# Branch projections of a hybrid decoder layer: from sixteen plain column tiles per set to four plain tiles and six pairs by seven block products

## The chip, the cores and the metric

The kernel runs on one core of a Trainium2 chip. The metric is the device time of one execution in microseconds; before the change the median of three runs is 3235.01 us (3234.76 to 3237.45).

## The reference, cut to what matters

One decoder layer on 576 tokens (512 of a prompt, 64 of samples), all in f32:

```python
u = einsum('bld,de->ble', rmsnorm(x, norm_w), w_in)        # z, xbc, dt, q, k, v, g_attn, mix_s, mix_a
y = gated_group_rmsnorm(ssd(conv(xbc), ...) + d_skip * xs, z)   # 576 x 4096
o = attention(q, k, v) * silu(g_attn)                           # 576 x 2048
p_ssm  = einsum('bli,id->bld', y, w_ssm_branch)                 # 4096 -> 2048
p_attn = einsum('bla,ad->bld', o, w_attn_branch)                # 2048 -> 2048
merged = sigmoid(mix_s) * p_ssm + sigmoid(mix_a) * p_attn
x = x + einsum('bld,de->ble', merged, w_out)
```

A final rmsnorm gives the outputs. This case is about `p_attn`, `p_ssm` and `merged`.

## The kernel before, in words

Everything is stored transposed: a tile has 128 features in the partitions and the tokens along the free axis, in two halves of 288 tokens. A product of f32 precision is made of three fp32r matmuls: a weight block W is split into `wh` (a copy on ACT, L75) and `wl` (a subtraction on DVE, L76), the activations likewise into `ah` and `al`, and TensorE adds `wh*ah + wh*al + wl*ah`. Weights come in chunks of 1024 x 128 (512 KB, `raw`, two buffers, L68), split into `wh`/`wl` (three buffers each).

There are two ways to multiply. **Plain** (`run_main`, matmuls at L338): a column tile of 128 output features has two chunks of 8 steps, and a step has three matmuls on each half of the tokens, so a tile is 2 x 8 x 3 x 2 = 96 matmuls of 288 columns. **Pairs** (`run_pairs`, matmuls at L442): two column tiles and the two halves of both the inputs and the tokens form a 2x2 block product that is done with seven block products instead of eight (the Winograd form of Strassen's method), each of 8 x 3 matmuls of 288 columns, so a pair is 168 matmuls where two plain tiles are 192. For it DVE makes four sums of weight blocks (S1 to S4, L382), seven weight blocks are split instead of four, and the results are put together by adds on eviction (L396, L401). The activation sums are made once per set of activations.

The order of the work: `FIRST` = 6 gate tiles ("mixes": sigmoid of one column tile of mix_a or mix_s, stored in DRAM as `ma_d`/`ms_d`), during which `sums_job` makes the activation sums; then 24 pairs for g_attn and z; then K, V, dt, and the four attention groups, with 13 mixes between them (`MIXES`); then the conv and scan groups, with 8 mixes between them (`MIXES_S`) and five behind the last. Attention and scan run as generators that are advanced by `pump()` after every step (lists `jobs`, paced, and `quick`, one advance per step), so that their small work lies between the matmuls; `drain()` at the end of a stage advances what is left. The tile scheduler puts instructions in order by program order and readiness, and each engine and each DMA queue then works strictly in that order.

Then the branch projections: `split_acts` loads o (16 row tiles of 128x576, L1261) and splits them into the 16 pairs `ah`/`al` (L1269 on ACT, L1270 on DVE); 16 plain tiles of `w_attn`; for each half of y the same, with 16 plain tiles of `w_ssm`. `gate` evicts: it loads the gate (L1329), multiplies on DVE (L1331, L1333) and adds into `mrg` (L1334), which stays in SBUF. So there are three sets of 16 plain tiles. Beside the first set the residual rows (`res_job`, L1308) and the final norm's weight `fw` (L1337) are loaded. Last come `w_out` (twice 16 plain tiles, one token span each), transposes, residual add and final norm.

## Time and profile before

| what | value |
|---|---|
| median of three runs | 3235.01 us (3234.76 to 3237.45) |
| the profiled execution | 3234.26 us |
| its span, first to last instruction | 3232.5 us |
| TensorE (PE) busy | 3145.6 us, 97% |
| VectorE (DVE) busy | 1782.0 us, 55% |
| ScalarE (ACT) busy | 1386.3 us, 43% |
| GpSimd (POOL) busy | 349.6 us, 11% |
| mean granted TensorE clock, as a share of full | 0.987 |
| bytes moved by DMA | 431.59 MB, mean 134 GB/s |

The busy share is an average over stages. A view by windows tells what an engine did in one stage (busy us, and in brackets the instructions), with the granted clock, the share of time that the 16 DMA engines were busy, and GB/s. In the chain of waits one follows what ended last back to the start.

### The profile page before, as it was taken

How to read it: one execution, taken by the hardware profiler on the slowest of the kernel's cores; microseconds unless marked ns; L12 is line 12 of the kernel's file. 1: busy time of each engine (PE TensorE's matmuls, PEld its weight loads, DVE VectorE, ACT ScalarE, POOL GpSimd, SP SyncE). 2: the span in 40 equal slices, each digit the busy share in tenths (PEclk: the TensorE clock that was granted, in tenths of full speed). 3: DMA queues.
4: the chain of work that ended last, by engine and by line, in shares of the span. 5: the costliest groups of instructions: out<-in, count | busy, mean ns of one | idle time of the engine just before them, and what ended most of it. 6: DMA issues, size and time to landing. Idle time of an engine off the chain costs nothing.

```text
span 3232.5 us, 57506 instructions
## 1 busy us (share of the span) xinstructions
PE 3145.6 (97%) x23323; PEld 3035.2 (94%) x23323; DVE 1782.0 (55%) x3076; ACT 1386.3 (43%) x2603; POOL 349.6 (11%) x427
## 2 busy tenths in 40 slices
PE   7989999999999999999999999999989999999997
PEld 6989999999989989999999999999879999999997
DVE  7656666632544443367776876866842333433454
ACT  5434444432455546445556555555531221212433
POOL 3200000000000100112122122122110000000111
PEclk9999999999999999999999999999999999999999
DMA  6564444433332432445645645645673443533555
GB/s 199 145 152 121 122 124 124 116 107 89 103 101 75 122 102 86 124 113 132 182 117 156 176 125 147 173 130 147 172 245 101 125 146 106 151 104 97 163 163 157
DMA packets 699272, 431.59 MB, mean 134 GB/s; under 512 B 41016, under 2 KB 663368, under 8 KB 698816
## 3 DMA queue, kind: packets, MB, share of 16 engines
q1 hardware_dynamic: 668000, 397.50, 44.3%
q10 hardware_dynamic: 18000, 18.35, 1.9%
q0 software_dynamic: 13008, 12.09, 1.5%
q8 instruction: 183, 3.00, 0.4%
q14 instruction: 81, 0.66, 0.1%
HBM read 363.37 MB, written 74.71 MB: 136 GB/s over the span
## 4 chain that ended last, share of the span: by engine, by line
PE 87%; DMA 6%; DVE 3%; ACT 2%; issue 1%; POOL 1%; SPq 0%; ACTq 0%; DVEq 0%; POOLq 0%
PE ps L338 60%; PE ps L442 16%; PE bank L637 1%; DMA raw<-in_w_out_dram 1%; PE bank L853 1%; PE bank L594 1%; DMA raw<-in_w_in_dram 1%; PE bank L1087 1%; PE bank L1065 1%; PE bank L627 1%; PE bank L923 1%; DVE wl L76 1%; PE bank L919 1%; ACT wh L75 1%; DMA L<-nacs_d 1%
## 5 line engine op out<-in xcount | busy, mean ns | idle before, releaser
L338 PE MATMUL ps<-ah,wh 128*128 128x288 f32 (+2 forms) x5408 | 1236.7, 300 | 25.4 <-ACT craw L816 9.6
L338 PE MATMUL ps<-ah,wl 128*128 128x288 f32 (+2 forms) x5408 | 1229.6, 299 | 2.0 <-DVE wl L76 1.8
L338 PE MATMUL ps<-al,wh 128*128 128x288 f32 (+2 forms) x5408 | 1229.9, 299 | 0.3 <-DVE al L1270 0.3
L75 ACT ACTIVATE wh<-raw 128x1024 fp32r<-128x1024 f32 x538 | 569.8, 1059 | 1232.7 <-PE ps L338 801.5
L76 DVE TENSOR_TENSOR wl<-raw,wh 128x1024 fp32r<-128x1024 f32 x538 | 670.2, 1246 | 689.1 <-ACT wh L75 685.9
L338 PEld LDWEIGHTS ps<-ah,wh 128*128 128x128 f32 x5408 | 897.7, 191 | 39.3 <-issue 17.8
L338 PEld LDWEIGHTS ps<-ah,wl 128*128 128x128 f32 x5408 | 897.9, 190 | 17.5 <-issue 10.8
L338 PEld LDWEIGHTS ps<-al,wh 128*128 128x128 f32 x5408 | 897.8, 190 | 5.1 <-issue 2.4
L442 PE MATMUL ps<-ah,wh 128*128 128x288 f32 x768 | 228.1, 297 | 6.3 <-DVE w L396 6.3
L442 PE MATMUL ps<-ah,wl 128*128 128x288 f32 x768 | 228.3, 297 | 2.0 <-DVE wl L76 2.0
L442 PE MATMUL ps<-al,wh 128*128 128x288 f32 x768 | 227.9, 297 | 0.0
L442 PEld LDWEIGHTS ps<-ah,wh 128*128 128x128 f32 x768 | 145.8, 190 | 6.5 <-issue 6.5
L832 DVE SCALAR_TENSOR_TENSOR cacc<-craw,prm,cacc 128x600 f32<-128x600 f32 x144 | 127.0, 887 | 42.1 <-ACT cacc L830 40.4
L442 PEld LDWEIGHTS ps<-ah,wl 128*128 128x128 f32 x768 | 145.7, 190 | 2.5 <-DVE wl L76 2.5
L442 PEld LDWEIGHTS ps<-al,wh 128*128 128x128 f32 x768 | 145.8, 190 | 0.1
L382 DVE TENSOR_TENSOR raw<-raw 128x1024 f32<-128x1024 f32 x96 | 117.0, 1221 | 46.3 <-DMA raw<-in_w_in_dram 45.4
L870 ACT ACTIVATE L<-L,nacs_n 128x128 f32<-128x128 f32 (+1 forms) x320 | 96.6, 379 | 61.0 <-DVE L L867 60.5
L1387 POOL TENSOR_TENSOR res<-res,fw 128x128 f32<-128x128 f32 (+3 forms) x35 | 31.7, 930 | 826.3 <-ACT junk L1383 793.1
L1333 DVE TENSOR_TENSOR sg<-ps,sg 128x576 f32<-128x576 f32 x32 | 24.2, 757 | 127.0 <-PE ps L338 127.0
L598 DVE CUSTOM_DVE_ANT_0 sc<-bank,bm 128x256 f32<-128x256 f32 (+1 forms) x128 | 43.8, 388 | 80.0 <-PE bank L594 72.1
L867 DVE TENSOR_TENSOR L<-L,nacs_n 128x512 f32<-128x512 f32 (+1 forms) x80 | 54.0, 691 | 51.7 <-DMA L<-nacs_d 51.1
L911 POOL TENSOR_TENSOR xl<-xe,xh 128x512 fp32r<-128x512 f32 x32 | 56.7, 1772 | 201.1 <-ACT xh L910 182.0
(508 smaller groups left out, 3664.3 us busy)
## 6 DMA issues: line engine op xcount, KB each, us to landing
raw<-in_w_in_dram SPq DMA_DIRECT2D x306, 512.0 KB
raw<-in_w_ssm_branch_dram SPq DMA_DIRECT2D x64, 512.0 KB
raw<-in_w_out_dram SPq DMA_DIRECT2D x64, 512.0 KB
L<-nacs_d SPq DMA_DIRECT2D x64, 256.0 KB
s<-in_state_ssm_dram SPq DMA_DIRECT2D x64, 256.0 KB
out_dram<-s SPq DMA_DIRECT2D x64, 256.0 KB
raw<-in_w_attn_branch_dram SPq DMA_DIRECT2D x32, 512.0 KB
zs<-z_d SPq DMA_DIRECT2D x32, 288.0 KB
```

The source lines that it names most:

```text
L75: pin(nc.scalar.activation(wh, raw, AF.Copy))
L76: pin(nc.vector.tensor_tensor(out=wl, in0=raw, in1=wh, op=ALU.subtract))
L338: ten.matmul(sums[i][:, s, :part.shape[1]], a[:, kk, :], part, start=(k == 0 and q == 0), stop=(k == last and q == 2))
L382: vec.tensor_tensor(out=s_[x], in0=s_[a], in1=s_[b], op=op)
L442: ten.matmul(st[p]["ps", i][:, :TH], a[:, k, :], b, start=i < 4 and k == 0 and q == 0, stop=k == 7 and q == 2, skip_group_check=i >= 4)
L594: ten.matmul(ps[:, i, lo:256], qT[m, h][:, blk * P:(blk + 1) * P], ks[h // 4][d][:, blk * P - 128 + lo:blk * P + P], start=d == 0, stop=d ...
L598: vec.tensor_tensor_reduce(out=s_[:, i, lo:256], in0=ps[:, i, lo:256], in1=bm[j][:, i, lo:256], scale=1.0, scalar=-3e38, op0=ALU.add, op1= ...
L627: ten.transpose(pt[:, r * P:(r + 1) * P], sc[j][:, i, kb * P:(kb + 1) * P], ident)
L832: vec.scalar_tensor_tensor(out=acc[:, :600], in0=raw[:, i:i + 600], scalar=prm[:, i * 48 + j:i * 48 + j + 1], in1=acc[:, :600], op0=ALU.mu ...
L867: vec.tensor_tensor(out=l_[:rows, :, :n], in0=l_[:rows, :, :n], in1=nacs_n[:rows, blk, h:h + 4].unsqueeze(2).to_broadcast([rows, 4, n]), o ...
L870: act.activation(l_[:rows, i, :n], l_[:rows, i, :n], AF.Exp, scale=-1.0, bias=nacs_n[:rows, blk, h + i:h + i + 1])
L911: pool.tensor_tensor(out=xl, in0=xe, in1=xh, op=ALU.subtract)
```

## The change

The three sets are done as four plain tiles (`FIRST_OUT` = 4) and six pairs each. `run_pairs` becomes `pairs_of`, which takes the weight and its first row and returns `head` (loads, two splits and three sums of the first pair) and `run`; `run_main` takes chunks loaded earlier (`raws`) and a callback `then` that it calls ahead of the last chunk. The activations are written into the tiles `hk` of the first stage (as `hx`), the activation sums are made anew for every set by `forms_job`, merged sums go by way of `mg_d` in DRAM, and the last two mixes (`N_END`) move from the attention stage to just ahead of the first set. The residual rows and `fw` are loaded at the start of `w_out`. The first 24 pairs keep their work; there `head` is called ahead of the last chunk of the six mixes, and the split of t1 comes behind the first product.

```diff
-MIXES = (2, 2, 3, 6)
-MIXES_S = (1, 1, 1, 1, 1, 1, 1, 1)
+MIXES = (2, 2, 2, 5)
+MIXES_S = (1, 1, 1, 1, 1, 1, 1, 0)
+N_END = 2
+FIRST_OUT = 4
...
+            if then and n == len(flat) - 2:
+                then()
...
-                st[p]["ps", i] = p1.tile([P, 512], F32, tag="ps", name="ps") if i < 4 else ...
+                    st[p]["ps", i] = p1.tile([P, 512], F32, tag=f"ps{i}", name="ps") if i < 4 else ...
...
+    raws = {}
+    run_main(seq, then=lambda: raws.update({0: W.load(in_loads(ends[0][0])[0])}))
+    drain()
+    stk, tx, rs, ev = pair_pools()
+    run_main([m_in(c, by_halves(gate_out(AF.Sigmoid, d_, n))) for c, d_, n in ends], raws=raws)
...
+    def acts_in(src, ks):
+        for k in ks:
+            t_ = staged_rows()
+            sync.dma_start(out=t_[:, :T], in_=src[k * P:(k + 1) * P, :])
+            split_half(hk[k], t_[:, :T])
...
+    def forms_job(src):
+        for k in range(8):
+            u, v = staged_rows(), staged_rows()
...
+            sync.dma_start(out=u1, in_=src[k * P:(k + 1) * P, :TH])
+            sync.dma_start(out=u2, in_=src[k * P:(k + 1) * P, TH:])
+            sync.dma_start(out=v[:, :T], in_=src[1024 + k * P:1024 + (k + 1) * P, :])
+            vec.tensor_tensor(out=t1_, in0=u2, in1=u1, op=ALU.subtract)
+            act.dma_start(out=xb_d[k * P:(k + 1) * P, :], in_=t1_)
+            vec.tensor_tensor(out=t2_, in0=v2, in1=t1_, op=ALU.subtract)
+            yield
+            split_half(tt[0][k], t2_)
+            pool.tensor_tensor(out=u2, in0=v2, in1=u2, op=ALU.subtract)
+            pool.tensor_tensor(out=v1, in0=v1, in1=t2_, op=ALU.subtract)
+            yield
+            split_half(tt[1][k], u2)
+            split_half(tt[2][k], v1)
+            yield
...
+    def merge_out(gate_d, n, add, last):
+        def f(j, src, t_):
...
+            sync.dma_start(out=sg, in_=gate_d[rows, cs])
+            if add:
+                mg = etile("mg")
+                sync.dma_start(out=mg, in_=mg_d[rows, cs])
+            vec.tensor_tensor(out=t_, in0=src, in1=sg, op=ALU.mult)
+            if add:
+                pool.tensor_tensor(out=t_, in0=t_, in1=mg, op=ALU.add)
+            if last and n > 13:
+                held.append((n, cs, t_))
+            else:
+                act.dma_start(out=mg_d[rows, cs], in_=t_)
...
+    def on_products(n, t1, raws, src, w, r0, rows):
+        def f(p, i):
+            if (p, i) == (-n, 0):
+                for k in range(8):
+                    split_half(b12[k], t1[k])
+            if p < -1:
+                return
+            if i in (1, 2):
+                raws[i - 1] = W.load(w_loads(w, r0, 0)[i - 1])
+            while i > 4 and held:
+                row, cs, t_ = held.pop(0)
+                split_half([a[:, cs] for a in hk[row]], t_)
+            if i == 2:
+                acts_in(src, range(4))
+            elif i == 3:
+                acts_in(src, range(4, 8))
+            elif i == 6:
+                acts_in(src, range(8, rows))
...
+    acts_in(o_d, range(KT))
+    for i in range(3):
...
+        def last_chunk():
+            head()
+            for k in range(8):
+                t1.append(etile("x"))
+                sync.dma_start(out=t1[k], in_=xb_d[k * P:(k + 1) * P, :])
...
+        quick.append(forms_job(src))
+        run_main([(w_loads(w, r0, n * P), hx, by_halves(takes[n])) for n in range(FIRST_OUT)], raws=raws, then=last_chunk)
+        drain()
...
+        run()
...
+    quick.append(res_job(xq, (0, 1, 2)))
+    sync.dma_start(out=fw, in_=AP(final_w, 0, [[0, P], [1, D]]))
-    oa = split_acts(staged)
...
-    run_main([(w_loads(w_attn[0], 0, n * P), oa, gate(ma_d, n, False)) for n in range(KT)])
-    for hk in range(2):
-        ya = split_acts([lambda k=k: load_act(y_d, 16 * hk + k) for k in range(KT)])
-        run_main([(w_loads(w_ssm[0], D * hk, n * P), ya, gate(ms_d, n, True)) for n in range(KT)])
```

The staged rows use the pairs' pool `rs` (five buffers of 4 KB a partition), the gates, merged sums and results the pool `ev` (14 tiles of 128x288). All 32 mixes are still made.

## Rows read from the trace of the kernel before

**Rows 1.** The page: TensorE's busy share, and its busy tenths in 40 slices.

```profile
PE 3145.6 (97%) x23323; PEld 3035.2 (94%) x23323; DVE 1782.0 (55%) x3076; ACT 1386.3 (43%) x2603; POOL 349.6 (11%) x427
...
PE   7989999999999999999999999999989999999997
```

**Rows 2.** The chain that ended last: start us, us, what, how many.

```profile
198.08 475.87 PE ps L442 x3574
...
717.69 12.80 PE ps L338 x96
...
2403.95 377.99 PE ps L338 x2820
```

**Rows 3.** Windows: us, busy us (instructions) per engine, clock, DMA share, GB/s.

```profile
core 0: us, PE busy (x) PEld busy (x) DVE busy (x) ACT busy (x) POOL busy (x), PEclk, DMA share, GB/s
198.00:674.00 476.00, 475.86 (x3574) 475.63 (x3574) 322.82 (x349) 197.61 (x265) 0.00 (x0) 0.99 0.43 122
...
2360.00:2380.00 20.00, 15.30 (x96) 14.28 (x96) 8.34 (x12) 10.63 (x18) 4.08 (x4) 0.91 1.05 357
2380.00:2404.00 24.00, 15.45 (x117) 15.25 (x115) 12.96 (x17) 8.34 (x11) 0.00 (x0) 0.87 0.87 262
...
2580.00:2604.00 24.00, 24.00 (x183) 24.00 (x182) 15.68 (x19) 11.99 (x16) 0.00 (x0) 1.00 0.81 258
...
2994.00:3014.00 20.00, 20.00 (x141) 19.98 (x140) 9.85 (x16) 7.47 (x10) 0.00 (x0) 1.00 0.61 191
```

**Rows 4.** Waits of TensorE, 2340 to 2420 us: total us, times, longest.

```profile
PE ps L338 <- DVE mrg L1331: 8.5, 1, 8.5
PE bank L977 <- ACT th L970: 3.5, 1, 3.5
```

**Rows 5.** Timeline of ACT, then of POOL, about the end of attention.

```profile
1310.01 0.65 ACT L1115 ACTIVATE mix<-ps 128x576 f32<-128x576 f32 x1
...
1340.87 0.41 ACT L814 ACTIVATE craw<-ps 128x288 f32<-128x288 f32 x1 [1.40 <-DMA o_d<-oT]
...
1330.25 6.54 POOL L653 TENSOR_TENSOR oT<-oT,ga 128x576 f32<-128x576 f32 x4 [11.89 <-DVE oT L737]
```

**Rows 6.** Groups by line and shape, 200 to 660 us: busy us, mean ns.

```profile
L76 DVE TENSOR_TENSOR wl<-raw,wh 128x1024 fp32r<-128x1024 f32 x146 | 178.4, 1223 | 82.5 <-ACT wh L75 82.5
L75 ACT ACTIVATE wh<-raw 128x1024 fp32r<-128x1024 f32 x145 | 153.9, 1062 | 266.2 <-PE ps L442 259.1 <-DMA z_d<-w 6.6 <-ACT w L1125 0.5
...
L382 DVE TENSOR_TENSOR raw<-raw 128x1024 f32<-128x1024 f32 x81 | 98.9, 1221 | 22.5 <-DMA raw<-in_w_in_dram 21.7
L396 DVE TENSOR_TENSOR c<-ps,u 128x288 f32<-128x288 f32 x42 | 19.1, 454 | 21.6 <-PE ps L442 21.6
```

**Rows 7.** Timeline of DVE, then of POOL, from 2350 us: start us, us.

```profile
2350.17 2.76 DVE L962 TENSOR_TENSOR xc<-xc,zs 128x576 f32<-128x576 f32 x4
...
2356.27 1.35 DVE L76 TENSOR_TENSOR wl<-raw,wh 128x1024 fp32r<-128x1024 f32 x1 [3.35 <-ACT wh L75]
...
2351.00 2.93 POOL L964 TENSOR_TENSOR tot<-xc 128x576 f32<-128x576 f32 x1 [31.90 <-DVE xc L962]
2353.89 1.14 POOL L964 TENSOR_TENSOR sqr<-xc 128x576 f32<-128x576 f32 x1
...
2356.62 2.01 POOL L964 TENSOR_TENSOR sqr<-xc 128x576 f32<-128x576 f32 x1
2358.71 1.42 POOL L966 TENSOR_TENSOR tot<-tot,sqr 128x576 f32<-128x576 f32 x1
```

**Rows 8.** DMA issues by line: how many, KB each.

```profile
raw<-in_w_ssm_branch_dram SPq DMA_DIRECT2D x64, 512.0 KB
...
stg<-y_d SPq DMA_DIRECT2D x32, 288.0 KB
...
x<-xb_d SPq DMA_DIRECT2D x8, 144.0 KB
```

**Rows 9.** Groups by line and shape, 2410 to 2990 us.

```profile
L1270 DVE TENSOR_TENSOR al<-stg,ah 128x576 fp32r<-128x576 f32 x32 | 23.2, 756 | 9.5 <-ACT ah L1269 9.4
L1269 ACT ACTIVATE ah<-stg 128x576 fp32r<-128x576 f32 x32 | 21.5, 684 | 16.7 <-DMA stg<-y_d 15.4
```

**Rows 10.** Groups by line and shape, DVE, 66 to 130 us.

```profile
L1166 DVE TENSOR_TENSOR x<-x 128x288 f32<-128x288 f32 x24 | 10.0, 453 | 0.0
```

**Rows 11.** Windows: 140 to 190 us alone.

```profile
140.00:190.00 50.00, 45.34 (x328) 44.65 (x326) 23.85 (x25) 16.86 (x22) 12.96 (x13) 0.97 1.04 222
```

More of the change, by code (lines that the diff above doesn't have):

```diff
@@ L308, in wait, with run_main @@
             yield
-    def run_main(tiles, had=()):
+    def run_main(tiles, had=(), raws={}, then=None):
         flat = [(i, c) for i, t in enumerate(tiles) for c in range(len(t[0]))]
@@ L322, in prep @@
                 i, c = flat[n]
-                ready[n] = W.split(W.load(tiles[i][0][c]))
+                ready[n] = W.split(raws.pop(n) if n in raws else W.load(tiles[i][0][c]))
         def step(n, kk, only=(0, 1)):
@@ L355, in run_main, with pairs_of @@
             n += m
-    def run_pairs(cols, ops, takes, after=None):
+    def pairs_of(w, r0, cols, ops, takes, after):
         n = len(cols)
@@ new lines, in head, with run @@
+        def head():
+            load(0, "A11", "A21", "A22", "A12")
+            split(0, 0)
+            sum_(0, "S1")
+            sum_(0, "S2")
+            split(0, 1)
+            sum_(0, "S3")
+        def run():
+            for p in range(n):
+                for i in range(7):
+                    if i < 5:
+                        split(p, i + 2)
+                    else:
+                        split(p + 1, i - 5)
+                    if i == 1:
+                        load(p + 1, "A11", "A21", "A22")
+                    elif i == 2:
+                        sum_(p, "S4")
+                    elif i == 3:
+                        sum_(p + 1, "S1")
+                        load(p + 1, "A12")
+                    elif i == 4:
+                        sum_(p + 1, "S2")
+                    elif i == 5:
+                        sum_(p + 1, "S3")
+                    st[p]["ps", i] = p1.tile([P, 512], F32, tag=f"ps{i}", name="ps") if i < 4 else st[p]["ps", (0, 2, 3)[i - 4]]
+                    wh, wl = st[p].pop(i)
+                    for k in range(8):
+                        ah, al = ops[i][k]
+                        for q, (a, b) in enumerate(((wh, ah), (wh, al), (wl, ah))):
+                            ten.matmul(st[p]["ps", i][:, :TH], a[:, k, :], b, start=i < 4 and k == 0 and q == 0,
+                                       stop=k == 7 and q == 2, skip_group_check=i >= 4)
+                        pump()
+                    evict(p, i)
+                    after(p - n, i)
@@ L449, in hybrid @@
+        return head, run
     win = w_in[0]
@@ L1173, in hybrid @@
     mixes = [(OFF_MA + n * P, ma_d, n) for n in range(16)] + [(OFF_MS + n * P, ms_d, n) for n in range(16)]
-    quick.append(sums_job())
-    run_main([m_in(c, by_halves(gate_out(AF.Sigmoid, d_, n))) for c, d_, n in mixes[:FIRST]], first)
-    drain()
-    ops[2] = [split_half(b12[k], t1[k]) for k in range(8)]
-    ms.close()
-    ms = ExitStack()
-    p1 = ms.enter_context(tc.tile_pool(name="p1", bufs=4, space=PSUM, reuse_waits="tile"))
     cols, takes = [], []
@@ L1230, in hybrid @@
     seq.append(m_in(OFF_DT, take_dt))
-    left = [m_in(c, take_mix(d_, n)) for c, d_, n in mixes[FIRST:]]
+    left = [m_in(c, take_mix(d_, n)) for c, d_, n in mixes[FIRST:-N_END]]
+    ends = mixes[-N_END:]
     for m in range(4):
@@ L1274, in hybrid, with w_loads @@
[L1274 to L1290 removed]
+    def w_loads(w, r0, col):
+        v = w[r0:r0 + D, col:col + P].rearrange("(c k p) n -> c p k n", p=P, k=8)
+        return [v[c] for c in range(2)]
@@ new lines, in hybrid @@
+    held = []
+    def merge_out(gate_d, n, add, last):
+        def f(j, src, t_):
+            rows, cs = slice(n * P, (n + 1) * P), slice(j * TH, (j + 1) * TH)
+            sg = etile("sg")
+            sync.dma_start(out=sg, in_=gate_d[rows, cs])
[7 more added lines that the diff above has]
+                held.append((n, cs, t_))
+            else:
+                act.dma_start(out=mg_d[rows, cs], in_=t_)
+        return f
```

165 lines of the change are left out of this document (64 added, 101 removed).

## The prediction

> **What bounds the kernel now.** I read the profile's page first. TensorE is busy for 97% of the span and is at 9 in nearly every slice [rows 1], so a change pays if it takes matmuls away or fills one of the few gaps, and costs what makes TensorE wait. The chain of waits says what one matmul of 288 columns costs: 12.80 us for the 96 of a plain tile, 133.3 ns each, and 475.87 us for 3574 in the pairs, 133.1 ns, the same price [rows 2]. The windows then show the stages. In the pairs TensorE waits for nothing while DVE is at 322.82 of 476 us (68%), ACT at 42% and DMA at a share of 0.43 [rows 3]. At the start of the second set, 2580 to 2604 us, 16 row tiles are loaded and split while DMA is at 0.81, and TensorE loses nothing. At the start of the first set it does: 96 and 117 matmuls in 44 us are worth 28.4 us at 133.3 ns, so 15.6 us are lost there [rows 3]. The view of waits names 12.0 us of it: 8.5 for an eviction that waits for its gate, 3.5 for the sum of squares of the last scan group [rows 4]; the rest is mostly a clock that was granted at 0.91 and 0.87 [rows 3].
>
> **The matmuls.** A pair has 168 instead of 192. Eighteen pairs drop 432, at 133.3 ns 57.6 us; per set 16 x 12.8 = 204.8 becomes 4 x 12.8 + 6 x 22.4 = 185.6 us. TensorE is the path here, so all of it counts: **-57.6 us**.
>
> **The start of the first set.** The two moved mixes are 2 x 12.8 = 25.6 us of matmuls whose inputs are there, put exactly where 15.6 us were lost. They cover the loading and splitting of o. What stays: the 3.5 us wait, because that small product is still ahead of later matmuls in TensorE's order, and I allow 2 us because the staging buffers take over memory of the scan stage, whose last y rows are still being stored. Bounds 0 and -15.6; I take **-10.1 us**.
>
> **The end of attention** loses those two tiles. The last mix left TensorE at 1310.0, the last gate products on POOL ended at 1336.8 and the next stage's first eviction came at 1340.9, held by the store of o [rows 5]. In between TensorE had two conv tiles (25.6 us) and the small attention products. Now 32 steps fewer, times 9/8, leave 36 more advances of the attention job to the drain: about one more block of queries. Its chain is mostly small work on ACT and DVE; the same two conv tiles cover it, and it can run beside the sample part. Bounds 0 and 25.6 (no cover at all); I take **+2 us**, near the first, since the block brings matmuls of its own.
>
> **The pairs of the three sets.** DVE per pair: 7 splits at 1.223, 4 weight sums at 1.221, 5 adds and 4 gate products at 0.454 us [rows 6]: 17.5 of 22.4 us, 78% against 68% in the pairs of before. ACT has 7 x 1.062 and one copy, under 8 us; it loses four evictions. POOL gets 4 adds, each half of the 1.42 us of a 576-wide one [rows 7]: 2.8 us. SP issues four weight loads and eight small ones; per pair 4 x 512 + 12 x 144 KB [rows 8] are 3.87 MB, 173 GB/s. ACT's queue issues 4 stores, and each waits for POOL's add, with the next weight splits queued behind it. Splits run two products (6.4 us) ahead, which covers an add that waits for DVE. The gate loads have 14 buffers, a pair's worth, so they are a pair ahead. Bounds 0 and 1 us per pair; I take **+3 us** over the 12 pairs that add.
>
> **The four plain tiles of a set** are the tight place: 51.2 us in which much else falls. DMA: 10 weight chunks (three tiles, and the head of the pairs), 8 row tiles of 288 KB, 8 x 576 KB for the activation sums, 8 x 144 KB stored and loaded again, and 8 x 144 KB each of gates, merged sums and results: 17792 KB = 18.2 MB, 356 GB/s. The best window here moved 357 at a share of 1.05; the second set's start, 258 at 0.81, would be 318 if full [rows 3]. At 318 it is 57.3 us, 6.1 too many. DVE has 8 x 0.756 for the rows [rows 9], 40 x 0.453 for sums and splits [rows 10], 10 x 1.223, 3 x 1.221 and 8 x 0.454 [rows 6]: 43.6 us, 85%. ACT, with 8 x 0.684 [rows 9], 24 half-size splits under 0.684 and 10 x 1.062, stays under 33 us. Part of the bytes can slip: rows come in during the last pair, weights are two or three chunks ahead, and the sums are due one product after the other. Bounds 0 and 6.1 per set, with an excess for the slower rates among the rivals. I take 4.5 for the sets with merged sums and 3 for the first: **+12 us**. SP works in order, so a load that waits for one of the five staging buffers holds the weight chunks behind it; that is how the excess reaches TensorE.
>
> **The boundary from pairs to tiles** I cost at nothing: the first eight row tiles come free after the third product and have 12.8 us, the accumulators of the first tile are evicted early, and the first two weight chunks are loaded during the last pair. Without that cover each set would start as the first did, 15.6 us. Dropping `mrg` and its 32 adds costs and brings nothing, since DVE had room there.
>
> **The output stage** gets 2560 KB of residual rows and 1024 KB of `fw` from the first set. A step takes three matmuls, 20 us / 141 each, 0.43 us [rows 3], so six loads nine steps apart spread 3.67 MB over 23 us: 158 GB/s on top of 191. That is 349 where 191 at a share of 0.61 would be 313 if full [rows 3], so about 2.6 us late. The first transposes also wait behind these jobs, with two result buffers. Bounds 0 and 8; **+3 us**.
>
> **The first pairs.** The loads come one chunk earlier, but the 140 to 190 us stretch is at a share of 1.04 from the bias table [rows 11], and that work is unchanged. Nothing, within 3 us.
>
> **Sum** against the profiled execution: 3234.3 - 57.6 - 10.1 + 2 + 3 + 12 + 3 = 3186.6; that execution is 0.75 us below the median, so I say **3187 us**.
>
> **Rival 1: DVE and POOL stand in each other's way.** POOL's square took 2.93 us while DVE multiplied from 2350.2 to 2352.9, and 2.01 beside a split, but 1.14 when free; that split took 1.35 instead of 1.223 [rows 6, 7]. So POOL stood still while DVE worked on two operands in SBUF, and DVE a little too. If their times simply add up, the four tiles have 43.6 + 24 x 0.71 = 60.6 us in the later sets (9.4 over) and 55.0 in the first (3.8 over), 22.6 instead of 12 us; a pair has 17.5 + 4 x 1.47 = 23.4, 1.0 over, 12 instead of 3 us. That gives 3187 + 19.6 = 3207 us. For it: these rows. Against: half of it can slip to where DVE has room. The Trainium skill (SBUF — State Buffer, Who interferes with whom) speaks against this change here: a DVE instruction with two SBUF inputs and a GpSimd instruction that reads SBUF exclude each other for the whole instruction. By that rule the times add up, and the trace agrees for POOL, with 2.93 against 1.14 us.
>
> **Rival 2: the row tiles come late** at the start of each set, in the staging buffers shared with the weights. Then each set starts as the first did: 3 x 15.6 = 46.8 instead of 12 + 5.5, so 3216 us. Against it: the loss-free second start [rows 3].
>
> **Rival 3: the drain of attention lies bare,** 25.6 instead of 2 us: 3211 us. For it: the eviction held by the store [rows 5].
>
> **Rival 4, slower: DMA at its poor rate.** In the stretch of the bias table DMA was full at 222 GB/s, and TensorE lost matmuls [rows 11]. At that rate the 18.2 MB of the four tiles take 82 us, 30.8 too many, 92 us in three sets: 3187 - 12 + 92 = 3267 us. It decides from 255 GB/s down: the gain without this term is 59.7, 19.9 per set, so break-even is at 71.1 us. For it: stores to DRAM and loads of short rows mix here too. Against it: 258 GB/s at a share of only 0.81 with the same row tiles [rows 3]. That the fewer matmuls are made and the time stays is the same case at its edge.
>
> **How the numbers follow.** Forecast 0.65 (3162 to 3200), rival 1 0.17, rival 2 0.08, rival 3 0.05, rival 4 0.05. All but rival 4 are faster; a little of rivals 2 and 4 ends near 3235. A measurement of this kernel tells about 0.2% (6.5 us) from no change: faster 0.91, same 0.04, slower 0.05. The range goes from 3162 (57.6 and 15.6 gained, nothing given back) to 3214, which takes in rivals 1 and 3 and leaves out most of rivals 2 and 4.
>
> **What would show it.** Right: 432 fewer matmuls of 288 columns; no waits over a microsecond inside the pairs; DVE near 78% there; the wait for `th` of some 3.5 us and no 8.5 us one at the first set; small waits of TensorE for weight splits or `ah`/`al` in the four tiles, with DMA near full. Wrong: pairs longer than 23 us with DVE full (rival 1), waits for `ah` at each set's first steps (rival 2), for `craw` about 1310 (rival 3), or four tiles of over 70 us with DMA full below 255 GB/s (rival 4).

## The result and the profile after

The changed kernel takes 3244.01 us (median of 15 runs, 3238.91 to 3251.81) against 3235.27 us (15 runs, 3231.99 to 3241.45) for the kernel before: a ratio of 1.0025, 95% interval 1.0016 to 1.0034. It is slower by 0.25%, and the prediction, 3187 us, is wrong in size and in sign. The profiled execution took 3241.34 us with a span of 3239.5, 7.0 us more than the 3232.5 of before.

The page of the changed kernel, busy time by engine:

```profile
## 1 busy us (share of the span) xinstructions
PE 3110.0 (96%) x22891; PEld 2986.3 (92%) x22891; DVE 2029.7 (63%) x3454; ACT 1481.7 (46%) x2773; POOL 487.8 (15%) x539
```

TensorE's busy time fell by only 35.6 us (3145.6 before, [rows 1]), though 432 matmuls are worth 57.6, and the span less this busy time is 129.5 us where it was 86.9. So part of the gain went into matmuls at a lower clock and the rest into waits. A ledger by stage says where. It is worked out from the starts of the matmuls of the two product lines in the trace (us; 19824 matmuls after, 20256 before, 432 fewer; "ideal" is 133.3 ns a matmul). The last two columns are experiments below; their profiled executions lie 4.8 us under and 6.3 us over the medians of their kernels, so the difference between these two columns, about 9 us, is smaller than that of the medians, 19.9.

| stage | before | after | ideal after | gates on ACT's queue | cover from the start |
|---|---|---|---|---|---|
| start to the first matmul of K | 674.6 | 669.8 | | 673.6 | 657.1 (two tiles fewer) |
| K to the first set (attention, scan, mixes) | 1693.2 | 1713.1 | | 1715.0 | 1727.1 (two tiles more) |
| first set, tiles + pairs | 217.3 | 53.6 + 136.0 | 51.2 + 134.4 | 55.4 + 136.5 | 53.7 + 137.5 |
| second set | 204.8 | 62.9 + 145.0 | 51.2 + 134.4 | 59.6 + 137.6 | 57.8 + 136.1 |
| third set | 205.1 | 57.0 + 147.8 | 51.2 + 134.4 | 56.2 + 135.7 | 58.6 + 136.0 |
| output stage, both spans | 225.2 | 241.8 | | 235.2 | 232.0 |

Four places ate the gain: the stretch from K to the first set is 19.9 us longer with the same matmuls in it; the tiles of the second and third set are 17.5 us over the ideal and their pairs 24.0; the output stage is 16.6 us longer. Only the first set behaves: it lost 12.5 us before (217.3 - 204.8) and loses 4.0 now.

The view by windows of the changed kernel (us busy, in brackets the instructions, then clock, DMA share, GB/s): the end of attention, the pairs of the first set, the tiles and pairs of the second, the start of the output stage.

```profile
1300.00:1350.00 50.00, 36.71 (x234) 32.81 (x233) 14.68 (x37) 16.34 (x45) 10.02 (x22) 0.76 0.24 69
...
2461.00:2572.00 111.00, 111.00 (x840) 111.00 (x839) 80.85 (x103) 42.41 (x47) 0.00 (x0) 1.00 0.54 159
2586.00:2635.00 49.00, 42.17 (x289) 41.76 (x288) 39.81 (x60) 19.23 (x37) 24.95 (x22) 0.90 0.92 274
2660.00:2780.00 120.00, 114.72 (x841) 112.92 (x840) 86.45 (x103) 42.20 (x48) 30.05 (x20) 0.99 0.58 174
...
2985.00:3030.00 45.00, 35.20 (x188) 32.40 (x187) 21.06 (x32) 14.88 (x21) 2.80 (x3) 0.85 0.87 267
```

The same stretch of attention in the kernel before had 324 matmuls in 45 us:

```profile
1300.00:1345.00 45.00, 45.00 (x324) 41.32 (x323) 13.65 (x39) 13.56 (x33) 8.61 (x16) 0.96 0.47 136
```

Read the two pairs rows together: 840 matmuls take 111.00 us in the first set, without a gap, and about 120 in the second. What the second has and the first has not is POOL's 20 sums and the merged loads that feed them; DVE is at 72 to 73% in both, DMA at 0.58 or less, so neither is full. At the end of attention and at the start of the output stage the clock is 0.76 and 0.85. At the end of attention the slow matmuls come ahead of the long wait, not behind it: from 1311 to 1322 us TensorE works on the last small matmuls of the attention, with no plain ones beside them, at a granted clock of 0.50 (1.2 GHz, the lower of its two levels). It had stood for 2.0 and 1.3 us just before. The 16 matmuls of one line take 5.5 us, where they took 3.5 in the kernel before:

```profile
1311.00:1322.00 11.00, 10.39 (x35) 8.15 (x34) 0.68 (x1) 0.45 (x1) 0.56 (x3) 0.50 0.17 48
...
L741 PE MATMUL bank<-pw,v 64*128 64x64 f32 x16 | 5.5, 445 | 0.4 <-DVE pw L736 0.4
...
L731 PE MATMUL bank<-pw,v 64*128 64x64 f32 x16 | 3.5, 296 | 0.0
```

With the 16 matmuls of the line before it (5.4 us against 3.4) that is 4 us. The wait that follows ends when the store of o has landed: it releases ACT's first eviction of a conv tile (`craw`), which fits buffers of the conv stage that lie where those of attention were. The eviction of the second conv tile comes right behind. So both conv tiles were done, the last plain matmul ahead of the wait stands at 1306 us, and with both accumulators full the third tile could not begin.

```profile
1330.80 0.41 ACT L824 ACTIVATE craw<-ps 128x288 f32<-128x288 f32 x1 [19.35 <-DMA o_d<-oT]
...
1331.45 0.43 ACT L824 ACTIVATE craw<-ps 128x288 f32<-128x288 f32 x1
```

TensorE's waits over the whole changed kernel:

```profile
PE ps L343 <- ACT craw L826: 15.8, 3, 9.4
PE ps L451 <- DVE wl L79: 14.9, 16, 1.7
...
PE ps L343 <- ACT wh L78: 6.7, 5, 2.7
PE ps L343 <- DVE o L1342: 6.5, 2, 4.7
PE ps L451 <- DVE w L402: 6.3, 2, 5.8
...
PE ps L343 <- DVE wl L79: 5.3, 10, 1.4
...
PE bank L987 <- ACT th L980: 4.8, 2, 4.1
```

The eviction that waited 8.5 us for its gate [rows 4] is gone, as forecast, and the wait for `th` stays. New are the 9.4 us for `craw` at the end of attention (between 1300 and 1350 us) and the waits of the pairs for a weight split `wl`: 13 of the 16, 12.3 us, lie in the second and third set.

### The profile page after: what moved, and what is told of

Its sections match the earlier page's. It is cut to its first block, busy times and chain, and to the rows that moved or that the text cites. A ratio compares the mean times of both kernels' runs of the same rounds, so it can differ in the third digit from the quotient of the medians.

```text
span 3239.5 us, 58401 instructions
## 1 busy us (share of the span) xinstructions
PE 3110.0 (96%) x22891; PEld 2986.3 (92%) x22891; DVE 2029.7 (63%) x3454; ACT 1481.7 (46%) x2773; POOL 487.8 (15%) x539
## 5 line engine op out<-in xcount | busy, mean ns | idle before, releaser
L79 DVE TENSOR_TENSOR wl<-raw,wh 128x1024 fp32r<-128x1024 f32 x592 | 746.1, 1261 | 538.8 <-ACT wh L78 520.5
L343 PE MATMUL ps<-ah,wh 128*128 128x288 f32 (+2 forms) x4256 | 992.1, 301 | 41.4 <-ACT craw L826 15.8
L343 PE MATMUL ps<-al,wh 128*128 128x288 f32 (+2 forms) x4256 | 985.8, 300 | 2.6 <-DVE al L1168 2.5
L343 PE MATMUL ps<-ah,wl 128*128 128x288 f32 (+2 forms) x4256 | 983.0, 300 | 5.3 <-DVE wl L79 5.3
L343 PEld LDWEIGHTS ps<-ah,wl 128*128 128x128 f32 x4256 | 712.1, 191 | 19.8 <-issue 8.5
L343 PEld LDWEIGHTS ps<-al,wh 128*128 128x128 f32 x4256 | 712.8, 191 | 11.6 <-issue 4.9
L451 PE MATMUL ps<-ah,wl 128*128 128x288 f32 x1344 | 401.5, 299 | 15.0 <-DVE wl L79 14.9
L451 PE MATMUL ps<-ah,wh 128*128 128x288 f32 x1344 | 400.2, 298 | 10.7 <-DVE w L402 6.3
L451 PE MATMUL ps<-al,wh 128*128 128x288 f32 x1344 | 399.4, 297 | 0.0
L451 PEld LDWEIGHTS ps<-ah,wl 128*128 128x128 f32 x1344 | 255.5, 190 | 19.5 <-DVE wl L79 19.3
L451 PEld LDWEIGHTS ps<-ah,wh 128*128 128x128 f32 x1344 | 255.4, 190 | 12.3 <-issue 11.2
L451 PEld LDWEIGHTS ps<-al,wh 128*128 128x128 f32 x1344 | 255.7, 190 | 0.1
L391 DVE TENSOR_TENSOR raw<-raw 128x1024 f32<-128x1024 f32 x168 | 205.3, 1224 | 77.0 <-DMA raw<-in_w_in_dram 41.0
L842 DVE SCALAR_TENSOR_TENSOR cacc<-craw,prm,cacc 128x600 f32<-128x600 f32 x144 | 126.1, 883 | 49.5 <-ACT cacc L840 47.9
L877 DVE TENSOR_TENSOR L<-L,nacs_n 128x512 f32<-128x512 f32 (+1 forms) x80 | 53.7, 688 | 56.0 <-DMA L<-nacs_d 55.8
```

What stands on the lines that cost most here:

```text
L79: pin(nc.vector.tensor_tensor(out=wl, in0=raw, in1=wh, op=ALU.subtract))
L343: ten.matmul(sums[i][:, s, :part.shape[1]], a[:, kk, :], part, start=(k == 0 and q == 0), stop=(k == last and q == 2))
L391: vec.tensor_tensor(out=s_[x], in0=s_[a], in1=s_[b], op=op)
L451: ten.matmul(st[p]["ps", i][:, :TH], a[:, k, :], b, start=i < 4 and k == 0 and q == 0, stop=k == 7 and q == 2, skip_group_check=i >= 4)
L842: vec.scalar_tensor_tensor(out=acc[:, :600], in0=raw[:, i:i + 600], scalar=prm[:, i * 48 + j:i * 48 + j + 1], in1=acc[:, :600], op0=ALU.mu ...
L877: vec.tensor_tensor(out=l_[:rows, :, :n], in0=l_[:rows, :, :n], in1=nacs_n[:rows, blk, h:h + 4].unsqueeze(2).to_broadcast([rows, 4, n]), o ...
```

## The experiments

All ratios are against runs of the kernel before on the same chip (its medians: 3235.17, 3235.08, 3235.33 and 3235.66 us in the four batches). Profiled runs of the changed kernel and its variants differ by some us in a stage that the edit did not touch (start to K: 668.7 to 674.5), so a stage of that length counts here only where it moved by more, or where a wait names it; differences of medians below some 4 us are not clear of the noise.

**The cover of the attention, from the tail.** The first theory for the 19.9 us: the two tiles that moved were the cover of the attention's last chain.

```diff
-MIXES = (2, 2, 2, 5)
+MIXES = (2, 2, 3, 6)
```

> Two mixes go back into the attention groups (2, 2, 3, 6); they are taken from the six behind the last scan group, so the two just ahead of the first set stay. Theory (bare drain: from the first matmul of the K tiles to the first one of the first set the changed kernel gained 5.7 us where two tiles are 25.6, so some 20 us were lost because the drain of the attention job has only two conv tiles beside it): the wait for craw about 1322 us (9.4) and the small ones around it are gone, and the kernel takes 15 to 20 us less than the changed kernel, 3224 to 3229 us. Rival (the scan stage lost them, or its tail needs the two tiles just as much): the time stays within 5 us of 3244, and the waits move to the end of the scan stage.

Measured: 3243.26 us (7 runs, ratio 1.0022, 1.0011 to 1.0033), no gain: the rival. TensorE's waits from 1290 to 2420 us say how:

```profile
PE ps L343 <- ACT ah L1167: 11.0, 1, 11.0
PE ps L343 <- ACT craw L826: 9.6, 3, 3.2
```

The 9.4 us wait is gone (three of at most 3.2 are left, as before the change), and an 11.0 us wait for the first split row stands at the start of the first set. With four tiles behind the last scan group instead of six, the drain of the scan lies bare in place of that of attention. Buffers for the conv outputs that need not wait for the store of o were not tried.

**The same, from the scan groups.**

```diff
-MIXES = (2, 2, 2, 5)
-MIXES_S = (1, 1, 1, 1, 1, 1, 1, 0)
+MIXES = (2, 2, 3, 6)
+MIXES_S = (1, 1, 1, 1, 1, 0, 0, 0)
```

> The attention gets back the two column tiles that the change took from it, at the cost of the sixth and seventh scan group instead of the tail (tail 6 and 2 ends as in the changed kernel). Theory A (the two tiles were the cover of the attention's drain, 18 to 20 us, and the tail is the cover of the scan's last group): the wait for craw of 9.4 us is gone, the start of the first set stays as in the changed kernel, and if the scan groups can spare a tile each the time falls by 15 to 20 us, to 3224 to 3229. Rival (all 32 tiles are needed as cover where they are, so that any move is a zero sum): the scan groups wait instead, the stretch from the keys to the two ends shortens by under 5 us, 3240 to 3246.

Measured: 3252.44 us (5 runs, 1.0052, 1.0039 to 1.0064), outside both: giving them from there costs more than it brings. Its waits of TensorE between 1300 and 2395 us:

```profile
PE bank L914 <- ACT xc L844: 11.6, 3, 9.5
PE ps L343 <- ACT craw L826: 11.5, 3, 7.4
```

The 9.4 us wait is gone here too, but the groups that lost their tile now wait: the transposes of the scan 9.5 us for a conv output, an eviction 7.4 us for `craw`.

**No tiles kept back at all** (run on the version with both queue edits below, 3224.07 us): all mixes as in the kernel before, nothing ahead of the first set.

```diff
-MIXES = (2, 2, 2, 5)
-MIXES_S = (1, 1, 1, 1, 1, 1, 1, 0)
+MIXES = (2, 2, 3, 6)
+MIXES_S = (1, 1, 1, 1, 1, 1, 1, 1)
...
-    run_main([m_in(c, by_halves(gate_out(AF.Sigmoid, d_, n))) for c, d_, n in ends], raws=raws)
```

> On the one with gates on ACT's queue and stores on POOL's: no column tiles are kept back for the start of the first set, all 32 mixes stand where the kernel before had them. Theory A (the two tiles bring as much at the first set as they cost in the attention): the stretch from the keys to the first set shortens by 18 to 20 us, the first set starts with its rows bare and loses 15 to 25 us: 3219 to 3231, the same. Rival 1 (the start of a set is not worth two tiles, as it lost only 12 us in the kernel before): 3210 to 3218. Rival 2 (with the buffers of the pairs opened before the rows can come in, the bare start costs more than before, 30 us or over): 3234 or more.

Measured: 3217.96 us (5 runs, 0.9949, 0.9936 to 0.9961), 6.1 us less than with the two tiles kept back. The time is in the band of rival 1, just under that of A; the bare start that A names is there. TensorE's waits from 1290 to 2420 us:

```profile
PE ps L343 <- ACT ah L1167: 18.0, 1, 18.0
PE ps L343 <- ACT craw L826: 9.9, 4, 3.2
```

So the two tiles cover 18.0 us at the first set, and moving them there uncovers about as much in the attention: in the changed kernel the move is worth nothing, or slightly less. But the 18.0 us are not those of the kernel before, where TensorE waited 0.8 us for `ah` there. That kernel issues the first eight loads of o during the last tiles (`stage_job`), the first of them 12 us ahead of the set's first matmul at 2367.7; the change leaves that out. Here all 16 stand on SP's queue behind four stores of y, which wait 9.5 us for the last scan group, and the first is issued 13.8 us after TensorE ran out of work at 2364.9. From the kernel before, then from this run:

```profile
2355.84 2.89 SPq L1261 DMA_DIRECT2D stg<-o_d  x2
...
2376.09 2.51 SPq L1002 DMA_DIRECT2D y_d<-xc  x4
2378.69 16.26 SPq L1304 DMA_DIRECT2D stg<-o_d  x16
```

The changed kernel with those early loads and no tiles moved was not run; it may need neither the cover nor its price.

**The cover of the attention, from the start** (with both queue edits and the residual edit below). Two of the six tiles that open the branch projections go to the attention.

```diff
-FIRST = 6
-MIXES = (2, 2, 2, 5)
+FIRST = 4
+MIXES = (2, 2, 3, 6)
```

> Store on POOL's queue, gate and merged loads on ACT's, residual rows spread out, and the two column tiles for the attention now taken from the six that open the branch projections, so that the scan keeps its seven and the tail its six and two. Theory A (the cover of the attention is worth 18 us wherever its tiles come from, and the start has room): the wait for craw of 9.4 us goes, no new wait in the scan, 3202 to 3210. Rival (zero sum: the six tiles at the start cover the loads and splits of the first pairs): the first stretch, from the start to the keys, keeps its 673 us although 25.6 us of matmuls left it, 3215 to 3228.

Measured: 3204.22 us (4 runs, 3198.82 to 3210.56; 0.9901, 0.9886 to 0.9916): theory A. Its nearest relative, the same kernel with the tiles taken from the scan groups (below), has 3225.64 us. By the ledger the start shrinks by 16.5 of the 25.6 us taken from it, and K to the first set grows by 12.1 for the 25.6 put there: the attention regains 13.5, the start pays 9.1. In the last experiment, which has the same order of mixes, the two stages take 655.4 and 1723.1 us: 17.5 regained and 7.4 paid. The profiled execution is the longest of the four runs here; by the medians the gain on the version with the two queue edits is 19.9 us, of which the residual edit has some 3, and the ledger shows only part of the rest. The wait for `craw` is 10.0 us in four pieces of at most 3.2, as expected.

**The store of the merged sum on POOL's queue.** In the changed kernel ACT's queue stores each merged sum, and the store waits for POOL's sum. What ACT waited for in the pairs of the second set, 2660 to 2780 us:

```profile
ACT wh L78 <- POOL c L1344: 27.3, 8, 5.7
ACT wh L78 <- PE ps L451: 23.2, 12, 4.8
ACT wh L78 <- POOL o L1344: 23.2, 4, 7.0
```

and its timeline (start, duration, instruction, idle time before it and its releaser):

```profile
2681.31 0.33 ACTq L1348 DMA_DIRECT2D mg_d<-w  x1
2683.05 0.33 ACTq L1348 DMA_DIRECT2D mg_d<-o  x1
2683.50 2.01 ACT L78 ACTIVATE wh<-raw 128x1024 fp32r<-128x1024 f32 x2 [5.90 <-POOL o L1344]
2690.48 0.33 ACTq L1348 DMA_DIRECT2D mg_d<-c  x1
2690.91 1.06 ACT L78 ACTIVATE wh<-raw 128x1024 fp32r<-128x1024 f32 x1 [5.40 <-POOL c L1344]
```

A weight split stands behind every store, and the store behind a product, its eviction on DVE and a sum on POOL. So ACT no longer runs two products ahead: it splits in a burst after each store. The store alone is not enough for that. In the first set the same four stores a pair stand in ACT's queue without a sum, ACT waits for DVE's evictions in front of splits, and TensorE loses nothing (2461 to 2572 us):

```profile
ACT wh L78 <- DVE c L402: 17.8, 5, 3.9
ACT wh L78 <- DVE w L1342: 15.3, 4, 4.4
```

What the later sets add is the sum: 50.5 of 120 us of ACT's waits end with POOL. And the two engines hold each other up here: the sums in front of the stores at 2681.31 and 2683.05, each begun after a weight split on DVE, take twice the 0.81 us of the sum that began before one, and there it is the split that takes 1.69 instead of 1.22 us. POOL, then DVE:

```profile
2679.61 1.67 POOL L1344 TENSOR_TENSOR w<-w,mg 128x288 f32<-128x288 f32 x1 [10.18 <-DVE w L1342]
2681.23 1.79 POOL L1344 TENSOR_TENSOR o<-o,mg 128x288 f32<-128x288 f32 x1
2689.64 0.81 POOL L1344 TENSOR_TENSOR c<-c,mg 128x288 f32<-128x288 f32 x1 [6.62 <-DVE c L1342]
...
2679.39 1.22 DVE L79 TENSOR_TENSOR wl<-raw,wh 128x1024 fp32r<-128x1024 f32 x1
...
2689.84 1.69 DVE L79 TENSOR_TENSOR wl<-raw,wh 128x1024 fp32r<-128x1024 f32 x1
```

```diff
-                act.dma_start(out=mg_d[rows, cs], in_=t_)
+                (pool if add else act).dma_start(out=mg_d[rows, cs], in_=t_)
```

> The stores of merged sums (sets two and three) are issued by POOL behind its own add, not by ACT. Theory (ACT stands at the store until POOL has added, and the next weight split stands behind it; wl comes late and TensorE waits): the twelve pairs of sets two and three, 145.0 and 147.8 us per six in the changed kernel, come to 134 to 137; the waits of TensorE for wl in the pairs (14.9 us, 16 times) nearly vanish; with the tiles' share some 20 to 25 us less, 3219 to 3224 us. Rival (DVE and POOL exclude each other, so the order of the store is not what matters): the pairs stay at 143 us or more, the time at 3240 to 3246.

Measured: 3231.85 us (10 runs, 0.9995, 0.9985 to 1.0004), 12.2 us less than the changed kernel. The pairs of sets two and three take 139.9 and 141.2 us (145.0 and 147.8), 11.7 less in all: over half the way to the 134 to 137 of the theory, and the time stays 8 us above its band. ACT's waits in 2660 to 2780 us are now

```profile
ACT wh L78 <- PE ps L451: 72.5, 33, 4.0
```

which is the healthy one: it is ahead, and waits for TensorE to let go of a buffer.

**The sum on DVE instead of POOL,** with the store left on ACT's queue:

```diff
-                pool.tensor_tensor(out=t_, in0=t_, in1=mg, op=ALU.add)
+                vec.tensor_tensor(out=t_, in0=t_, in1=mg, op=ALU.add)
```

> The sum of a gated product with the merged sum so far goes from POOL to DVE; stores stay on ACT's queue. Theory A (ACT's weight splits queue behind a store that waits for a POOL add which is slow beside DVE): the wait of ACT for POOL goes, as it did when the store moved to POOL's queue; DVE has 4 x 0.45 us more per pair, but its own products no longer stand beside a POOL sum. The pairs of sets two and three take 139 to 141 us each instead of 145.0 and 147.8, the whole about 3230 to 3235. Theory B (the lost time in the pairs is DVE running out of time, whoever stores): DVE gets fuller, the pairs stay at 145 to 150 us or grow, 3242 to 3255.

Measured: 3238.37 us (10 runs, 1.0013, 1.0003 to 1.0023), between the two; the pairs take 140.5 and 144.4 us, shorter with a fuller DVE (in the shortest of the ten runs, 6.1 us under the median). So DVE's own time is not what limits the pairs. The edit takes away POOL's sum and its slowing beside DVE together, so it does not tell the order on ACT's queue from the two engines in each other's way; the last experiment, which leaves the sum on POOL, and the next one speak for the order. The store still waits for a product's eviction there, only for a shorter time.

**Gate and merged loads on ACT's queue,** on top of the store on POOL's:

```diff
-            sync.dma_start(out=sg, in_=gate_d[rows, cs])
+            act.dma_start(out=sg, in_=gate_d[rows, cs])
...
-                sync.dma_start(out=mg, in_=mg_d[rows, cs])
+                act.dma_start(out=mg, in_=mg_d[rows, cs])
```

> On top of the store on POOL's queue, the loads of gates and merged sums go to ACT's queue, so that they no longer stand behind weight chunks and staged rows on SP. Theory A (what remained in the pairs, 5 to 7 us a set, was DVE waiting for late gates, 15.1 us in one stretch of 120 us): that wait goes, the pairs of sets two and three take 135 to 137 us each (139.9 and 141.2 with the store moved alone), and the first tiles of the output stage shorten since the last gates come in time: 3214 to 3224 in all. Rival (DVE and POOL in each other's way is what is left): pairs stay at 139 to 141 us, the whole at 3228 to 3235. A third way: the loads now hold ACT's splits where a buffer is not free yet, and the pairs grow.

Measured: 3224.07 us (5 runs, 0.9962, 0.9949 to 0.9975), 7.8 less again, just over the upper end of A. The pairs after the first one of a set now run without a gap beside POOL's sums, in 2666 to 2777 us:

```profile
2666.00:2777.00 111.00, 111.00 (x840) 111.00 (x839) 86.87 (x103) 43.97 (x50) 38.63 (x40) 1.00 0.63 190
```

The reason that I gave is only half shown. DVE still waits 7.4 us for gates in this stretch (15.1 in the version before it, over 120 us), and in the first set of the changed kernel it waits 15.3 us for them without a loss. What the edit also does is to clear SP's queue, where a load that waited for its buffer held the weight chunks behind it. Which of the two counted was not told apart.

**The forms of the rows on DVE.** Of the sums for the seven products two per row tile are POOL's:

```diff
-            pool.tensor_tensor(out=u2, in0=v2, in1=u2, op=ALU.subtract)
-            pool.tensor_tensor(out=v1, in0=v1, in1=t2_, op=ALU.subtract)
+            vec.tensor_tensor(out=u2, in0=v2, in1=u2, op=ALU.subtract)
+            vec.tensor_tensor(out=v1, in0=v1, in1=t2_, op=ALU.subtract)
```

> The sixteen activation sums per set that POOL makes are made by DVE. Theory (a POOL sum of 0.9 to 1.0 us holds a DVE instruction of 0.45 us up to 1.05, so sums on POOL cost DVE more than making them there): DVE instructions of 288 in the four tiles are back at 0.45 us, and the four tiles of sets two and three, 62.9 and 57.1 us, come to 53 to 56; 6 to 12 us less in all, 3232 to 3238. Rival (the four tiles are held by DMA, near 290 GB/s there, or by DVE's own work, 16 x 0.45 = 7.3 us more now): the tiles stay at 57 to 63 us and the time within 4 us of 3244.

Measured: 3244.38 us (6 runs, 1.0029, 1.0018 to 1.0041), no difference to the changed kernel as a whole, as the rival has it. The tiles of sets two and three take 58.5 and 56.0 us (62.9 and 57.0), 5.4 less, but their pairs stay at 146.3 and 146.5, and the gain is lost again in the output stage (245.0 us, from 241.8) and in stages that the edit does not touch.

**No sums on POOL at all:** the last two edits for DVE together, on the version with both queue edits.

> As the one with gates on ACT's queue and stores on POOL's, but every sum of the sets (merged sums, and the forms of the rows in the four tiles) is on DVE, POOL only stores. Theory A (what is left in the four tiles, 8.4 and 5 us over 51.2 in sets two and three, is DVE slowed by POOL's sums beside it): the tiles take 53 to 56 us each, the pairs stay at 136 to 138; 3215 to 3222 in all. Rival (it is DVE's sheer work, or the transfers): 24 sums of 0.45 us more on DVE in the tiles make them 62 to 70 us, 3225 to 3245.

Measured: 3217.74 us (4 runs, 0.9947, 0.9933 to 0.996), as A expected: tiles 55.3 and 53.2 us (59.6 and 56.2 with POOL), 7.3 less, although DVE has more to do. The pairs take 138.5 and 141.3, 0.5 and 3.3 us above that band: the first pair of a set takes 27.2 and 30.0 us (26.3 and 24.4), so a part is given back. In the changed kernel's timeline the contention can be seen at work:

```profile
2599.66 1.04 DVE L1320 TENSOR_TENSOR stg<-stg 128x288 f32<-128x288 f32 x1
2600.62 0.44 DVE L1342 TENSOR_TENSOR o<-ps,sg 128x288 f32<-128x288 f32 x1
...
2601.59 1.05 DVE L1168 TENSOR_TENSOR t12l<-stg,t12h 128x288 fp32r<-128x288 f32 x1
2602.56 0.45 DVE L1322 TENSOR_TENSOR stg<-stg 128x288 f32<-128x288 f32 x1
```

and POOL beside it:

```profile
2599.38 1.00 POOL L1325 TENSOR_TENSOR stg<-stg 128x288 f32<-128x288 f32 x1
2600.34 1.00 POOL L1326 TENSOR_TENSOR stg<-stg 128x288 f32<-128x288 f32 x1
2601.32 1.01 POOL L1325 TENSOR_TENSOR stg<-stg 128x288 f32<-128x288 f32 x1
```

A DVE sum of two SBUF tiles takes 0.45 us alone and 1.04 or 1.05 beside a POOL sum. The gate product at 2600.62, whose first input is in PSUM, keeps its 0.44 beside one.

**The residual rows spread out.** They are loaded at the start of the output stage; here the first span's loads stay where the program has them, and the second span's come 100 steps later.

```diff
-                sync.dma_start(out=res[b][:, qs], in_=rows_of(*toks[b], x_prompt, x_sample)[:, qs])
+                pin(sync.dma_start(out=res[b][:, qs], in_=rows_of(*toks[b], x_prompt, x_sample)[:, qs]))
...
-    quick.append(res_job(ep, (3, 4)))
+    jobs.append(res_job(ep, (3, 4), 100))
```

> The residual loads are pinned into program order on SP, so that they are spread over the first tiles of w_out as the code spaces them, and those of the second span come 100 steps later, beside the other list. Theory (ten loads of up to 512 KB and the 1 MB of the norm's weight are issued in one lump, and the weight chunks queue behind them): the first three tiles of w_out, 13.5, 12.4 and 13.8 us against 7.0, 7.0 and 7.7 before, come to 7 to 9 each; 11 to 16 us less, 3228 to 3233. Rival (the late row tiles of merged sums and their splits, or the two result buffers with the transposes behind them, hold those tiles): at most 5 us less.

Measured: 3240.62 us (10 runs, 1.002, 1.001 to 1.0029), 3.4 less: in the rival's band, and not clear of the noise. The first three tiles of the output stage take 13.5, 11.1 and 7.4 us (13.5, 12.4 and 13.8 in the changed kernel, 7.0, 7.0 and 7.7 before): the lump of residual rows holds the third; the first two are held by something else.

**Four edits together:** the diffs above for the store, the loads, the residual rows, and the tiles from the scan groups.

> The store on POOL's queue, gate and merged loads on ACT's, the two column tiles given back to the attention from the scan groups, and the residual rows spread out. If the four causes are separate (attention 18, pairs 12, late gates 8, residual rows 5 us), they add up to some 40 us: 3200 to 3210, faster than both kernels. If the attention's tiles are a zero sum: 3215 to 3225. If the gates don't matter either: 3225 to 3232.

Measured: 3225.64 us (5 runs, 0.9967, 0.9954 to 0.998), just above the band for a zero sum of the attention's tiles, and no better than the two queue edits alone: K to the first set took 1723.9 us (1715.0), by the same waits as with the tiles taken from the scan groups alone, and the output stage's gain (232.9 us, from 235.2) is lost in that.

**The residual rows in the order of their use,** on the best version. There DVE still stood at the output sum, between 2955 and 3035 us:

```profile
DVE wl L79 <- ACT wh L78: 27.9, 15, 3.2
DVE res L1451 <- DMA res<-in_x_sample_dram: 4.3, 1, 4.3
```

```diff
-        for b in which:
-            for q in range(2):
+        for q in range(2):
+            for b in which:
...
-    sync.dma_start(out=fw, in_=AP(final_w, 0, [[0, P], [1, D]]))
+    jobs.append(fw_job())
```

> On the one with the cover taken from the start: the residual rows come in the order in which they are used (the first halves of all three blocks, then the second halves), and the final weight comes late, before its first use. Theory A (what still holds the first tiles of the output stage is DVE standing at the sum with the third block's rows, 4.3 us, which come as the fifth load, and loads that compete with the chunks of the output weights): tiles 2 and on take 7.0 to 7.5 us, the first 9 to 12, the first span 117 to 121 us (126.1 with the cover from the start, 117.5 in the kernel before), the whole 3195 to 3201. Rival (the first tile waits for its rows, and the clock is at half for what follows, whatever comes beside): the first span stays at 124 to 128 us, the whole at 3201 to 3207.

Measured: 3204.36 us (5 runs, 0.9905, 0.9891 to 0.992), the same as without: the rival. The wait for `res` is gone from that view, yet the first span takes 126.2 us (126.1). Its first tile takes 11.8 us, in a stretch where DMA is full and the clock not:

```profile
2961.00:2975.00 14.00, 10.60 (x59) 9.59 (x57) 7.48 (x12) 5.81 (x9) 2.05 (x2) 0.88 1.05 308
```

The wait that was taken away covered another. In 2955 to 2975 us TensorE waits for split rows of the merged sums, four times in all:

```profile
PE ps L343 <- DVE al L1168: 1.8, 2, 1.2
PE ps L343 <- ACT ah L1167: 1.6, 2, 0.9
```

The tile begins at 2957.37 and needs all 16 rows; of the 14 that come back from DRAM, ACT splits the last four only from 2957.89 to 2964.89. Whether these waits, and the clock of 0.50 behind them (2966 to 2969 us), make up the 4.8 us by which this tile is longer than the 7.0 of the kernel before was not tested.

## Why the prediction was wrong

**The matmuls: right.** 432 fewer, and the clean pairs take 22.25 us where I had 22.4.

**The start of the first set: right in size, partly by luck.** Its loss fell from 12.5 to 4.0 us (2.4 of them in its tiles, counted again below), 8.5 where I took 10.1. But I took the bare start for that of the kernel before; the change had also dropped the early loads of o, and without the tiles TensorE stands 18.0 us there. What the tiles covered was mostly a gap of the change's own.

**"The same two conv tiles cover it": this step failed,** +19.9 us instead of +2. I had named the full price, 25.6, as the upper bound and as the third rival, gave that 0.05, and argued it away with the two conv tiles and the block's own matmuls. But the conv tiles were spent ahead of the chain's end: both were done by 1306 us, and no third could begin until the store of o had landed, just ahead of 1330.80. The attention's own matmuls brought no cover either: the last 32, alone, ran at a clock of 0.50 for 11 us, which made the chain 4 us longer, and then TensorE stood 9.4 us. Two tiles beside that chain end both: in the six experiments that put them back, TensorE waits for nothing between 1290 and 1400 us. And two of the three places that I took tiles from had none to spare: the tail gave nothing, the scan groups lost 8, and only the start paid (13.5 to 17.5 us of gain for 7.4 to 9.1 of cost).

**"Splits run two products (6.4 us) ahead, which covers an add that waits for DVE": this step failed,** 24.0 us instead of 3 in the pairs with merged sums. I had the store, the sum and the splits behind it in the right order, but saw the store as waiting for one add. It waits for a product, its eviction and the add, four times a pair, with the next splits behind it. Up to the eviction the first set has the same waits and loses nothing; with the add behind it the lead is used up. Moving the store alone gave 11.7 us back, moving the loads as well another 7.8. The first rival, DVE and POOL in each other's way, had the right place and at most a part of the cause: pairs longer than 23 us, but with DVE at 72%, and free of loss beside POOL's sums, but for the first pair of a set, once the queues were changed; POOL's adds beside DVE, 1.67 to 1.79 us where I had 0.71, lengthen the wait of the store. The rival's price for the pairs was also added up wrongly: 4 x 1.47 takes half of the 2.93 us that already hold the waiting, and with the 0.71 of the tiles a pair is 17.5 + 2.8 = 20.3 us, which fits.

**The four plain tiles: the mechanism was right, the term mis-sized,** 2.4, 11.7 and 5.8 us instead of 3, 4.5 and 4.5. With no sum on POOL the tiles of sets two and three stay 4.1 and 2.0 us over the ideal, which fits the transfers that I summed (not shown apart from DVE's work), and the contention of the first rival comes on top: taking POOL's sums out of the tiles gave 5.4 and 7.3 us. I had let that stand as a rival, 22.6 us over the three sets, where 19.9 were measured; as a term of its own it belonged into the sum.

**The boundary from pairs to tiles: right.** The first tiles of sets two and three take 13.65 and 14.19 us, 2.2 us in all over 12.8 each (counted in the tiles).

**The output stage: this step failed,** 16.6 us instead of 3 and beyond my bound of 8. I priced the bytes only, and the loss is order. The lump of residual rows stood in SP's queue among the weight chunks, the loads of gates and merged sums stood late in it, and the clock was low, 0.85 in the first 45 us. Spreading the rows gave 2 to 6 us of the stage (241.8 to 236.1 alone, 235.2 to 232.9 with the other edits), the loads on another queue 6 (241.0 to 235.2). The wait of DVE for the residual rows, which I took for another part, was worth nothing. 6.8 us were not won back (232.0 against 225.2), and their cause stays open: the late rows of the merged sums at the first tile are the candidate.

**The fourth rival,** DMA at its poor rate, gave the right side for the wrong reason: the tiles of the second set moved 274 GB/s at a share of 0.92, well above 222, and the attention's and the pairs' losses, the larger ones, lie where DMA is at a share of 0.24 and 0.58.

The sum: -57.6 - 8.5 + 19.9 + 17.5 + 24.0 + 16.6 is +11.9; the start, which the change hardly touches, came out 4.8 us shorter in this execution, and 7.1 is what the spans show (7.0).

With the store and the loads on other queues the change does pay: 3217.96 us with all tiles where the kernel before has them, 0.995 of it. With the residual rows spread and two tiles from the start put ahead of the first set it is 3204.22 us, 0.99; whether the kernel before would gain from those two tiles as well was not run.

## What to carry to other kernels

A DMA issue is an instruction in its engine's order (a store stood 5.90 us in front of the weight splits here): put the store of a late result on a queue that has nothing else to do ahead of TensorE, and not in front of the work that keeps TensorE fed; and keep loads that could go early ahead of stores that must wait. A matmul tile that is moved to cover one gap leaves the gap that it covered; before it is counted as a gain, find the wait that ends last where it came from. And where a term has two bounds, an argument for the low one should name the instruction that does the covering and its length, not only its kind.

## What was not expected of the hardware

A DVE sum of two SBUF tiles is itself slowed, from 0.45 to 1.05 us, beside a POOL sum; in the rows of before only POOL had shown it clearly [rows 7]. In the lines shown the one that began later is held: the DVE sum at 2599.66 behind the POOL sum at 2599.38, but the POOL sum at 2679.61 (1.67 us) behind the DVE split at 2679.39. One input from PSUM is enough to escape, with 0.44 us. The Trainium skill (SBUF — State Buffer, Who interferes with whom) says that a DVE instruction with at most one SBUF input, outside the modes that use both port pairs, does not contend with GpSimd; the trace agrees with that number.

A thin stretch costs TensorE more than its gaps: at the end of attention the clock stood at 0.50 while TensorE did 11 us of small matmuls ahead of the 9.4 us wait, and the matmuls of one line took 445 ns each instead of 296.
